# The closing projection of a two-layer decoder step: first halves of three chunks ahead, the last chunk's halves exchanged, and one more weight set in page buffers

## The chip, the cores and the metric

The kernel runs on one core of a Trainium2 chip. The metric is the device time of one execution in microseconds (us). Engines are named as in the profile: PE is TensorE (PEld its weight loads), DVE is VectorE, ACT is ScalarE, POOL is GpSimd, SP is SyncE, which here only issues DMAs.

## The reference

One inference step of a small decoder with two layers, on a prompt of 512 tokens and 8 sampled sequences of 8 new tokens, model width 1024. Layer 0 is a gated DeltaNet, layer 1 a differential attention over shared keys and values. What matters here is the last thing that is computed, the output projection of layer 1 with its gated residual:

```
def diff_mixer(h, k_all, v_all, ...):
    q, z = jnp.split(h @ w_in, [DIFF_WIDTH], axis=-1)
    ...
    o = rms_norm(o, sub_gain) * (1.0 - lam_init)
    o = o * jax.nn.silu(z.astype(F32)).reshape(b, L, DIFF_HEADS, DIFF_VH)
    return o.reshape(b, L, DIFF_WIDTH).astype(h.dtype) @ w_out

# run_group, layer 1
x = x + gate[:, None, :] * y
```

The matrix `w_out` is 1024 x 1024, and 512 + 64 = 576 tokens go through it.

## The kernel before, in words

Activations lie transposed: partitions are model components, columns are tokens. The 576 columns are cut in two halves of 288: half 0 is prompt tokens 0 to 287; half 1 is prompt tokens 288 to 511 (224 columns) and the 64 sample tokens. A matrix of 1024 x 1024 is cut into 8 chunks m of 128 outputs, and each chunk is a sum over 8 blocks k of 128 inputs; for the output projection, block k is head k.

Float32 products are made of three float32r products. Weights and activations are each split into a high part (a cast) and a low part (the value less the high part): `hhi` and `hlo` for activations, and a weight set of `whi` and `wlo` for a chunk. For each k, `run_part` issues hi x hi, hi x lo and lo x hi, so a half chunk is 24 matmuls of 288 columns into one PSUM bank.

A weight set j is loaded raw by SP into one of two `wraw` buffers (`weights`). Then `split_w` casts it on ACT (L2025) and subtracts twice 512 columns on POOL (L2031), or on DVE for some sets that the change does not touch. Where the two parts go is a table: for most late sets it is a slot of the room "w2", which has two, and which comes free when the chunk that uses it is done. Sets named in `OVER` go to two page buffers `pg`, which held key and value pages of the cache and which are no longer needed then. The closing projection uses sets 40 to 47; chunk m uses set 40 + m.

The activations of the closing projection come from `gated2`: for each head the attention output is multiplied by the gate (L2677, DVE), cast to `hhi` (L2682, ACT) and subtracted to `hlo` (L2684, DVE). It sets ("g", h, half) for the prompt part, and ("gs", 1) for the sample part of all heads, which comes from `samples_end`. So half 0 of a chunk needs ("g", k, 0), and half 1 needs ("g", k, 1) and ("gs", 1).

`out_second` (L2800) is the closing projection. It goes through a list `order` of (m, half). The first `HELD` entries are held: their blocks k 0 to 6 are issued first, each into its own bank, and the blocks k 7 of all of them after that, since head 7 is the last to be done. The other entries follow one after another. Banks go round in the order of `names`: pq, px, px, po, sc, sc, pt2, pv. `xin` loads the residual input for each entry of `order` into one of three `scr` buffers (L2812). `evac` adds the product times the gate (one DVE operation for half 0, three for half 1: `resid`, L1829, L1833, L1835) and stores the result (L2826); its buffer comes free when the store has landed. Half 1 leaves the weight set.

What sets the order of instructions on an engine is not this text alone. All pieces of work are generators that are driven by a planner (`Second.drive`) with costs for each step. It takes the step that can start first by its own clock, and by rank where two are equal; the order that it finds is then pinned on PE, ACT, DVE, POOL and SP. Each engine takes its instructions in that order, and each waits for what it needs.

Of the kernel before, what the change touches and what calls it, by code (L numbers as in the profile page):

```python
# [170 lines left out]
def scr(K, n):  # L171
    t = K.scr.tile([128, 640], F32, name="scr")
    return t[:, 0:n]
# [714 lines left out]
SPARE = 1.4  # L888
HALF = 8, 20
PAGES_AT = 1, 7  # L890
HELD = 4
EV = 3
BURST = 4
MORE = 2
OVER = 40,
CH = 3
PB = 3

# [925 lines left out]
def resid(K, pool, half, ps, m, gate_kt, xin, xout):  # L1824

    nc = K.nc
    g = K.mod[:, gate_kt + m, :]
    n = HT if half == 0 else SEQ - HT
    nc.vector.scalar_tensor_tensor(out=xout[:, :n], in0=ps[:, :n], scalar=g[:, 0:1], in1=xin[:, :n],  # L1829
                                   op0=ALU.mult, op1=ALU.add)  # L1830
    if half:
        t = pool.tile([128, NB, DS], F32, name="rst")
        nc.vector.tensor_mul(out=t[:], in0=ps[:, n:HT].rearrange("p (b e) -> p b e", e=DS),  # L1833
                             in1=g[:, 1:9].unsqueeze(2).to_broadcast([128, NB, DS]))
        nc.vector.tensor_add(out=xout[:, n:HT], in0=xin[:, n:HT], in1=t[:].rearrange("p b e -> p (b e)"))  # L1835
# [162 lines left out]
def weights(W, K, first, n, slot):  # L1998


    for j in range(first, first + n):
        room = "w" if j < 24 else "wx" if j == 26 and EV > 2 else "pg" if j in OVER else "w2"
        yield None, 0, Room("raw")
# [32 lines left out]
def run_part(W, K, j, ps, half, ks, step=2, conds=lambda k: ()):  # L2036

    ks = list(ks)
    for i in range(0, len(ks), step):
        now = ks[i:i + step]  # L2040
        yield "E", None, ("w", j), *[c for k in now for c in conds(k)]
        w = W.sets[j]
        for k in now:
            for a, b in ((0, 0), (0, 1), (1, 0)):
                K.mm(out=ps[:, :HT], lhsT=w[a][:, k, :], rhs=(K.hhi, K.hlo)[b][:, k, half * HT:half * HT + HT],
                     start=(k == 0 and a + b == 0), stop=(k == 7 and a == 1))
# [307 lines left out]
def second_projections(W, K):  # L2354
# [75 lines left out]
    yield from tile_row(W, K, [Tile2(W, K, "v", h) for h in range(8)], 24, "v", [nothing] * 2)  # L2430
    yield from tile_row(W, K, [Tile2(W, K, "z", h) for h in range(8)], 32, "z", named("hz"))
    yield from out_second(W, K)


# [365 lines left out]
def out_second(W, K):  # L2800


    P = W.P
    order = [(m, half) for m in range(8) for half in range(2)]
    xs = {}

    def xin():
        for m, half in order:
            yield None, 0, Room("scr"), ("z", 7, 0), ("z", 7, 1)
            t = scr(K, HT)  # L2810
            xs[m, half] = t, W.took[0]
            K.nc.sync.dma_start(out=t, in_=K.x1d[:, m, CUTS[half]])  # L2812
            W.load("S", 0.5, "xo", m, half)
            W.set("xol", m, half)

    def evac(m, half, bank):
        nc = K.nc
        ps, took = bank
        yield None, 0, ("xol", m, half)
        x, xr = xs[m, half]  # L2820
        yield "D", 0.52 if not half else 0.9, ("xo", m, half)
        y = x
        resid(K, P.ss, half, ps, m, 56, x, y)
        W.leave(took)
        yield None, 0
        nc.sync.dma_start(out=K.yT[:, m, CUTS[half]], in_=y)  # L2826
        W.load("S", 0.5, "yo", m, half)
        yield None, 0, ("yo", m, half)
        W.leave(xr)

    W.add(6, xin())
    def conds(half):
        return lambda k: (("g", k, half),) + ((("gs", 1),) if half else ())
    held = []
    names = ["pq", "px", "px", "po", "sc", "sc", "pt2", "pv"]
    for (m, half), name in zip(order[:HELD], names):
        yield None, 0, Room(name), *((("gs", 1),) if name in ("px", "po") else ())
        bank = getattr(K, name).tile([128, 512], F32, name=name), W.took[0]
        yield from run_part(W, K, 40 + m, bank[0], half, range(7), conds=conds(half))
        held.append(bank)  # L2840
    for (m, half), bank in zip(order[:HELD], held):
        yield from run_part(W, K, 40 + m, bank[0], half, (7,), conds=conds(half))
        W.add(0, evac(m, half, bank))
        if half:
            W.leave(*W.sets[40 + m][2])
    for i, (m, half) in enumerate(order[HELD:]):
        name = names[(i + HELD) % 8]
        yield None, 0, Room(name)
        bank = getattr(K, name).tile([128, 512], F32, name=name), W.took[0]
        yield from run_part(W, K, 40 + m, bank[0], half, range(8), conds=conds(half))  # L2850
        W.add(0, evac(m, half, bank))
        if half:
            W.leave(*W.sets[40 + m][2])
# [368 lines left out]
```

## Time and profile before

| | |
|---|---|
| runs | 1150.34, 1156.87, 1158.28 us; median 1156.87 |
| span of the profiled execution | 1149.0 us; its own device time is not listed apart from the span, and the lowest run is 1.3 us above it |
| busy share of the span | PE 97%, DVE 60%, ACT 60%, POOL 38% |
| granted TensorE clock | 0.995 on average |
| chain that ended last | PE 78%, ACT 7%, DVE 5%, DMA 5% |
| last matmul | starts at 1144.83 us of the span |

In the timelines a row is: start, duration, engine, line, operation, output <- inputs, shapes, and in brackets the idle time of the engine before it and what ended that. Names of tiles are without their numbers there, and the bank pt2 is printed as pt. In a table of windows each engine has its busy time in the window with the number of its instructions; then come the granted clock (1.00 is full), the busy share of the DMA engines and GB/s.

### The profile page before, as it was taken

How to read it: one execution, taken by the hardware profiler on the slowest of the kernel's cores; microseconds unless marked ns; L12 is line 12 of the kernel's file. 1: busy time of each engine (PE TensorE's matmuls, PEld its weight loads, DVE VectorE, ACT ScalarE, POOL GpSimd, SP SyncE). 2: the span in 40 equal slices, each digit the busy share in tenths (PEclk: the TensorE clock that was granted, in tenths of full speed). 3: DMA queues.
4: the chain of work that ended last, by engine and by line, in shares of the span. 5: the costliest groups of instructions: out<-in, count | busy, mean ns of one | idle time of the engine just before them, and what ended most of it. 6: DMA issues, size and time to landing. Idle time of an engine off the chain costs nothing.

```text
span 1149.0 us, 32501 instructions
## 1 busy us (share of the span) xinstructions
PE 1118.5 (97%) x12651; PEld 1036.0 (90%) x12651; DVE 694.6 (60%) x1803; ACT 693.9 (60%) x1901; POOL 439.4 (38%) x752
## 2 busy tenths in 40 slices
PE   8999999999999999999999999999999999999998
PEld 6899998999989998998989999999998888888988
DVE  4677875777777675866743657564433456555522
ACT  4666867777777867677753434685553566665510
POOL 3443433323334334232223432389962223422412
PEclk9999999999999999999999999999999999999989
DMA  9886565767657675686886889322589988988434
GB/s 366 214 231 165 143 199 133 192 155 198 166 139 192 145 206 142 179 215 163 234 239 160 273 287 341 124 59 74 182 305 328 312 295 324 317 275 302 154 99 125
DMA packets 87643, 239.97 MB, mean 209 GB/s; under 512 B 14450, under 2 KB 28658, under 8 KB 87490
## 3 DMA queue, kind: packets, MB, share of 16 engines
q1 hardware_dynamic: 71938, 181.27, 46.5%
q0 software_dynamic: 15552, 56.63, 22.6%
q8 instruction: 100, 1.64, 0.6%
q14 instruction: 53, 0.43, 0.1%
HBM read 212.02 MB, written 25.84 MB: 207 GB/s over the span
## 4 chain that ended last, share of the span: by engine, by line
PE 78%; ACT 7%; DVE 5%; DMA 5%; issue 3%; POOL 2%; SPq 1%; POOLq 0%; ACTq 0%; DVEq 0%
PE pp L271 24%; PE pp L1930 12%; PE pc L271 7%; PE pq L1930 7%; PE px L1930 4%; PE po L1930 3%; PE pa L271 3%; PE sc L1930 3%; PE pt L1935 3%; PE pt L271 3%; PE pt L1930 2%; PE pv L1930 2%; PE ps L271 2%; DMA whi<-wall 2%; PE pt L285 1%
## 5 line engine op out<-in xcount | busy, mean ns | idle before, releaser
L271 PE MATMUL pp<-hlo,whi 128*128 128x288 f32 x592 | 170.6, 309 | 0.0
L271 PE MATMUL pp<-hhi,whi 128*128 128x288 f32 x592 | 162.1, 294 | 0.0
L2031 POOL TENSOR_TENSOR wlo<-wraw,whi 128x512 fp32r<-128x512 f32 x80 | 108.6, 1371 | 137.5 <-ACT whi L2025 131.5
L1930 PE MATMUL pp<-hhi,whi 128*128 128x288 f32 x432 | 133.0, 309 | 2.4 <-DVE rst L1833 1.7
L1930 PE MATMUL pp<-hlo,whi 128*128 128x288 f32 x432 | 127.2, 295 | 0.0
L1930 PE MATMUL pp<-hhi,wlo 128*128 128x288 f32 x432 | 125.6, 295 | 0.0
L271 PE MATMUL pp<-hhi,wraw 128*128 128x288 f32 x576 | 123.8, 298 | 0.0
L271 PEld LDWEIGHTS pp<-hlo,whi 128*128 128x128 f32 x592 | 111.5, 188 | 1.8 <-issue 1.4
L271 PEld LDWEIGHTS pp<-hhi,whi 128*128 128x128 f32 x592 | 111.6, 188 | 0.5
L271 PE MATMUL pp<-hhi,wlo 128*128 128x288 f32 x592 | 103.5, 303 | 0.0
L271 PEld LDWEIGHTS pp<-hhi,wraw 128*128 128x128 f32 x576 | 94.0, 189 | 1.0 <-issue 0.4
L1930 PEld LDWEIGHTS pp<-hhi,whi 128*128 128x128 f32 x432 | 81.4, 188 | 6.8 <-issue 4.5
L1134 DVE SCALAR_TENSOR_TENSOR y<-u,vec,y 128x600 f32<-128x600 f32 x96 | 80.7, 841 | 9.4 <-ACT y L1131 8.7
L271 PEld LDWEIGHTS pp<-hhi,wlo 128*128 128x128 f32 x592 | 84.6, 188 | 0.8 <-issue 0.2
L271 PE MATMUL pp<-hlo,wraw 128*128 128x288 f32 x288 | 84.4, 314 | 0.1
L1930 PEld LDWEIGHTS pp<-hlo,whi 128*128 128x128 f32 x432 | 81.5, 189 | 0.0
L1930 PEld LDWEIGHTS pp<-hhi,wlo 128*128 128x128 f32 x432 | 80.8, 188 | 0.0
L2025 ACT CAST whi<-wraw 128x1024 fp32r<-128x1024 f32 x46 | 48.2, 1049 | 51.1 <-PE po L1930 18.1
L926 POOL DMA_DIRECT2D wlo<-wall x36 | 32.0, 890 | 118.7 <-ACT wlo L921 74.8
L2490 POOL COPY pg<-ptt 1x1 int32<-1x1 int32 x128 | 27.3, 224 | 125.8 <-PE po L1930 45.5
L1930 PE MATMUL pq<-hhi,whi 128*128 128x288 f32 x200 | 65.0, 325 | 0.6 <-ACT vch L2247 0.4
L1930 PE MATMUL pq<-hlo,whi 128*128 128x288 f32 x200 | 58.9, 295 | 0.0
(492 smaller groups left out, 3127.2 us busy)
## 6 DMA issues: line engine op xcount, KB each, us to landing
pg<-ck SPq DMA_DIRECT2D x64, 512.0 KB, 5.3
pg<-cv SPq DMA_DIRECT2D x64, 512.0 KB, 5.3
wraw<-wall SPq DMA_DIRECT2D x49, 512.0 KB, 4.4
wraw<-wall POOLq DMA_DIRECT2D x36, 512.0 KB, 6.0
whi<-wall POOLq DMA_DIRECT2D x36, 512.0 KB, 5.9
wlo<-wall POOLq DMA_DIRECT2D x36, 512.0 KB, 5.9
araw<-ada SPq DMA_DIRECT2D x24, 512.0 KB, 4.2
araw<-ada SPq DMA_DIRECT2D x8, 1024.0 KB, 13.8
```

The lines of the kernel that those rows point to most:

```text
L271: return self.K.nc.tensor.matmul(**kw)
L285: return self.K.nc.tensor.transpose(**kw)
L926: K.nc.gpsimd.dma_start(out=lo[:], in_=src, accum_op=ALU.add)
L1134: nc.vector.scalar_tensor_tensor(out=y[:, :YW], in0=u[:, j:j + YW], scalar=cw[j], in1=y[:, :YW], op0=ALU.mult, op1=ALU.add)
L1930: return self.K.nc.tensor.matmul(**kw)
L1935: return self.K.nc.tensor.transpose(**kw)
L2025: nc.scalar.copy(out=hi[:], in_=raw[:])
L2031: (nc.vector if shared else nc.gpsimd).tensor_sub(out=lo[:, q:q + 4], in0=raw[:, q:q + 4], in1=hi[:, q:q + 4].bitcast(F32))
L2490: nc.gpsimd.tensor_copy(out=e, in_=P.ptt[0:1, i:i + 1])
```

## The change

Four places, all in the closing projection and its tables. Three entries are held, not four, and they are the first halves of chunks 0, 1 and 2; their second halves follow. The last chunk's second half comes ahead of its first half. The banks go round in another order, and the two sc banks are taken only when the prompt's last attention product is issued (("pv", 7, 3)); the px and po banks no longer ask for ("gs", 1) themselves, while the second halves still wait for it. Set 43 goes to page buffers as set 40 does. Since no held entry is a second half, the release of a weight set goes from that loop.

```
-HELD = 4
+HELD = 3
...
-OVER = 40,
+OVER = 40, 43
...
-    order = [(m, half) for m in range(8) for half in range(2)]
+    order = [(m, half) for half in range(2) for m in range(HELD)] + [(m, half) for m in range(HELD, 7) for half in range(2)] + [(7, 1), (7, 0)]
...
-    names = ["pq", "px", "px", "po", "sc", "sc", "pt2", "pv"]
+    names = ["pq", "sc", "sc", "px", "px", "po", "pt2", "pv"]
     for (m, half), name in zip(order[:HELD], names):
-        yield None, 0, Room(name), *((("gs", 1),) if name in ("px", "po") else ())
+        yield None, 0, Room(name), *((("pv", 7, 3),) if name == "sc" else ())
         bank = getattr(K, name).tile([128, 512], F32, name=name), W.took[0]
         yield from run_part(W, K, 40 + m, bank[0], half, range(7), conds=conds(half))
         held.append(bank)
     for (m, half), bank in zip(order[:HELD], held):
         yield from run_part(W, K, 40 + m, bank[0], half, (7,), conds=conds(half))
         W.add(0, evac(m, half, bank))
-        if half:
-            W.leave(*W.sets[40 + m][2])
```

The order of instructions up to the middle of the closing projection's first chunk is the same on every engine. On PE, the first two blocks below begin with the end of chunk 0's first half up to head 6 (bank pq, set 40 in two pg tiles) and what follows it. Before, it is the second half of the same chunk:

```order
L1930 MATMUL pq_17218<-hhi_102,pg_17024 128x288
L1930 MATMUL pq_17218<-hlo_103,pg_17024 128x288
L1930 MATMUL pq_17218<-hhi_102,pg_17025 128x288
L1930 MATMUL px_17282<-hhi_102,pg_17024 128x288
L1930 MATMUL px_17282<-hlo_103,pg_17024 128x288
L1930 MATMUL px_17282<-hhi_102,pg_17025 128x288
```

Now it is the first half of chunk 1 (bank sc, set 41):

```order
L1930 MATMUL pq_17218<-hhi_102,pg_17024 128x288
L1930 MATMUL pq_17218<-hlo_103,pg_17024 128x288
L1930 MATMUL pq_17218<-hhi_102,pg_17025 128x288
L1930 MATMUL sc_17270<-hhi_102,whi_17169 128x288
L1930 MATMUL sc_17270<-hlo_103,whi_17169 128x288
L1930 MATMUL sc_17270<-hhi_102,wlo_17170 128x288
```

So 42 matmuls of sc, 21 for each of chunks 1 and 2, have come between pq and px. The second place on PE is where the held banks get head 7. Before, four are closed, and the first half of chunk 2 follows (bank sc, set 42):

```order
L1930 MATMUL pq_17218<-hhi_102,pg_17024 128x288
L1930 MATMUL pq_17218<-hlo_103,pg_17024 128x288
L1930 MATMUL pq_17218<-hhi_102,pg_17025 128x288
L1930 MATMUL px_17282<-hhi_102,pg_17024 128x288
L1930 MATMUL px_17282<-hlo_103,pg_17024 128x288
L1930 MATMUL px_17282<-hhi_102,pg_17025 128x288
L1930 MATMUL px_17304<-hhi_102,whi_17169 128x288
L1930 MATMUL px_17304<-hlo_103,whi_17169 128x288
L1930 MATMUL px_17304<-hhi_102,wlo_17170 128x288
L1930 MATMUL po_17326<-hhi_102,whi_17169 128x288
L1930 MATMUL po_17326<-hlo_103,whi_17169 128x288
L1930 MATMUL po_17326<-hhi_102,wlo_17170 128x288
```

Now three are closed, and only then comes the first second half, that of chunk 0 in bank px:

```order
L1930 MATMUL pq_17218<-hhi_102,pg_17024 128x288
L1930 MATMUL pq_17218<-hlo_103,pg_17024 128x288
L1930 MATMUL pq_17218<-hhi_102,pg_17025 128x288
L1930 MATMUL sc_17270<-hhi_102,whi_17169 128x288
L1930 MATMUL sc_17270<-hlo_103,whi_17169 128x288
L1930 MATMUL sc_17270<-hhi_102,wlo_17170 128x288
L1930 MATMUL sc_17307<-hhi_102,whi_17225 128x288
L1930 MATMUL sc_17307<-hlo_103,whi_17225 128x288
L1930 MATMUL sc_17307<-hhi_102,wlo_17226 128x288
L1930 MATMUL px_17345<-hhi_102,pg_17024 128x288
L1930 MATMUL px_17345<-hlo_103,pg_17024 128x288
L1930 MATMUL px_17345<-hhi_102,pg_17025 128x288
```

Head 7 has moved from behind 63 matmuls of second halves to behind 42 of first halves, and the first use of the sample columns to behind 51. On ACT, the piece of the difference at the end of its program (L2682 are the casts of activations, 8x64 the sample columns of all heads; L2025 are the casts of weight sets):

```order
 L2682 CAST hhi_102<-qT_9616 128x224 x7
 L2682 CAST hhi_102<-qT_9616 128x288
+L2025 CAST pg_17278<-wraw_17212 128x1024
 L2682 CAST hhi_102<-qT_9616 128x8x64
 L2682 CAST hhi_102<-qT_9616 128x224
-L2025 CAST whi_17366<-wraw_17212 128x1024
-L2025 CAST whi_17436<-wraw_17272 128x1024
-L2025 CAST whi_17505<-wraw_17410 128x1024
-L2025 CAST whi_17575<-wraw_17481 128x1024
-L2025 CAST whi_17645<-wraw_17552 128x1024
```

Set 43's cast has moved from behind the last casts of activations to ahead of the sample columns' cast. On POOL its two subtractions have moved along. They follow those of set 42 as before, and wait for the cast. On DVE the order of the hlo subtractions is the same.

## The prediction

> **What bounds the kernel now.** The page first.
>
> ```profile
> span 1149.0 us, 32501 instructions
> PE 1118.5 (97%) x12651; PEld 1036.0 (90%) x12651; DVE 694.6 (60%) x1803; ACT 693.9 (60%) x1901; POOL 439.4 (38%) x752
> PEclk9999999999999999999999999999999999999989
> PE 78%; ACT 7%; DVE 5%; DMA 5%; issue 3%; POOL 2%; SPq 1%; POOLq 0%; ACTq 0%; DVEq 0%
> ```
>
> TensorE is busy for 97% of the span and is 78% of the chain that ended last. The change keeps all its matmuls, so it can win only where TensorE stands still or runs slowly, and behind its last matmul. There is one clock slice below 9, the last but one. Next the list of TensorE's waits, by what ended them (total, times, longest):
>
> ```profile
> PE px L1930 <- ACT hhi L2682: 3.7, 1, 3.7
> PE px L1930 <- DVE hlo L2684: 0.3, 1, 0.3
> ```
>
> The longest single wait of the kernel, and a short one right behind it, lie at bank px, the second half of chunk 0, which needs the sample columns of hhi and hlo. The timeline of TensorE around it, to its end (start, duration), and the same stretch in windows (us, busy time of PE, PEld, DVE, ACT, POOL, then clock and DMA):
>
> ```profile
> 1089.97 0.29 PE L1930 MATMUL pq<-hhi,pg 128*128 128x288 f32 x1
> 1093.95 0.61 PE L1930 MATMUL px<-hhi,pg 128*128 128x288 f32 x1 [3.68 <-ACT hhi L2682]
> 1094.87 0.61 PE L1930 MATMUL px<-hlo,pg 128*128 128x288 f32 x1 [0.32 <-DVE hlo L2684]
> ...
> 1099.46 0.29 PE L1930 MATMUL px<-hhi,pg 128*128 128x288 f32 x1
> 1099.59 0.29 PE L1930 MATMUL px<-hhi,whi 128*128 128x288 f32 x1
> ...
> 1144.83 0.29 PE L1930 MATMUL pv<-hhi,wlo 128*128 128x288 f32 x1
> ```
>
> ```profile
> 1090.10:1092.45 2.35, 0.16 (x2) 0.00 (x0) 2.35 (x5) 0.22 (x1) 0.73 (x1) 1.00 0.25 37
> 1092.45:1099.28 6.83, 5.01 (x19) 4.70 (x20) 2.67 (x7) 0.90 (x2) 0.00 (x0) 0.50 0.18 64
> 1099.28:1145.12 45.84, 45.84 (x346) 45.61 (x344) 10.33 (x29) 5.24 (x5) 12.67 (x10) 1.00 0.42 126
> ```
>
> From the first px chunk after the gap to the end there are 342 matmuls by the code (21 of (1,0), 21 of (1,1), 12 that close the four held chunks, 12 x 24): 1099.59 to 1144.83 is 45.24 us for 341 steps, **0.1327 us a matmul**, without a wait. The idle stretch also brought the clock down: 0.50 for 6.83 us. So the closing projection is TensorE alone, at full pace except at that one place.
>
> **What the gap costs.** At full pace the matmul behind 1089.97 would start at 1090.10. It starts at 1093.95, which is 3.85 late. The next starts 0.92 behind it, so 0.79 over a step. From there to 1099.46 are 19 steps in 4.59 us, where full pace needs 2.52: 2.07 for the half clock. Together **6.71 us**.
>
> **What the change puts there.** Ahead of px now stand 42 matmuls of the first halves of chunks 1 and 2 (k 0 to 6) and nine that close the three held chunks. Their operands: first-half columns of k 0 to 6 were read by pq already. The lower part of set 42 is the later weight: the POOL rows below end at 1090.83, and PE comes to that set after 21 steps, at 1092.89. The condition that ("pv",7,3) be done only delays the sc banks to the end of the prompt's attention; its conversions are what pq just read. So 42 steps run from 1090.10 without a wait, then the first of chunk 0's k 7 starts at 1095.67, and the second, which reads hlo of head 7, could start at 1095.81.
>
> **What the change adds in the gap.** Set 43 goes to two page buffers, so its cast on ScalarE now stands between the last first-half cast and the sample cast, and its two POOL subtractions fall in the gap.
>
> ```profile
> 1084.83 0.34 SPq L2006 DMA_DIRECT2D wraw<-wall  x1
> wraw<-wall SPq DMA_DIRECT2D x2, 512.0 KB, 3.7
> 1086.99 1.04 ACT L2025 CAST whi<-wraw 128x1024 fp32r<-128x1024 f32 x1
> 1089.89 0.43 ACT L2682 CAST hhi<-qT 128x288 fp32r<-128x288 f32 x1
> 1093.28 0.90 ACT L2682 CAST hhi<-qT 128x512 fp32r<-128x512 f32 x2 [2.95 <-DVE qT L2677]
> ```
>
> ScalarE is idle for 2.95 us there. The raw weights, issued at 1084.83 with 3.7 us to landing, are in at about 1088.5. The cast runs from 1090.32 to 1091.36 and ends before the sample cast can start, 1093.28. On ScalarE it costs nothing. On POOL and VectorE it does not hide, and this I take from the timeline of set 42, whose subtractions met the same VectorE work:
>
> ```profile
> 1088.11 1.33 POOL L2031 TENSOR_TENSOR wlo<-wraw,whi 128x512 fp32r<-128x512 f32 x1 [1.14 <-ACT whi L2025]
> 1088.34 1.35 DVE L2684 TENSOR_TENSOR hlo<-qT,hhi 128x224 fp32r<-128x224 f32 x1
> 1089.40 1.43 POOL L2031 TENSOR_TENSOR wlo<-wraw,whi 128x512 fp32r<-128x512 f32 x1
> 1089.61 1.46 DVE L2684 TENSOR_TENSOR hlo<-qT,hhi 128x224 fp32r<-128x224 f32 x1
> 1091.66 0.37 DVE L2684 TENSOR_TENSOR hlo<-qT,hhi 128x224 fp32r<-128x224 f32 x1
> 1093.77 0.45 DVE L2684 TENSOR_TENSOR hlo<-qT,hhi 128x288 fp32r<-128x288 f32 x1
> 1094.14 0.68 DVE L2684 TENSOR_TENSOR hlo<-qT,hhi 128x512 fp32r<-128x512 f32 x1
> ```
>
> Alone an hlo subtraction of 224 columns takes 0.37. Beside a POOL subtraction it takes 1.35 and 1.46, ending 0.25 behind it. Two held ones cost 1.35 + 1.46 - 2 x 0.37 = 2.07 us (the same figure as the half clock by chance). The new POOL pass starts at about 1091.44 and lies over the hlo operations from 1091.66 on, so I shift that whole chain by 2.07: hlo of head 7 is done at 1094.22 + 2.07 = 1096.29 and its matmul starts 0.05 later (1094.82 to 1094.87 above), at 1096.34, against 1095.81. **TensorE waits 0.53 us.** That is far from the 2.35 us of idling (1090.10 to 1092.45) after which the clock fell, so it stays at 1.00. Behind it come eight steps, so px starts at 1097.40; the sample cast (first of the two in its row, which with the shift are done at 1096.25) and its hlo (1094.82 + 2.07 = 1096.89) are there. Bounds: 0 if the two passes do not meet, and 1.4 if each costs a full 1.46 (2 x 1.46 = 2.92, 0.85 more than 2.07).
>
> The Trainium skill, page "SBUF — State Buffer", section "SBUF: two separate sides", says that a VectorE operation with two SBUF inputs and a GpSimd operation exclude each other, whichever starts first keeping the shared ports for its whole instruction. It speaks against placing set 43's subtractions here, and the rows agree (1.35 and 1.46 instead of 0.37). By that rule the sum has the 0.53, without it the gain would be 0.53 larger.
>
> **What is moved and costs nothing.** SP's load of set 45 now stands ahead of the first stores and waits for set 43's subtractions (about 1094.2); the first evacuation can start when the hlo chain is done, at about 1097.2 (1094.82, one more of 0.37, and the 2.07), and its store after that, so nothing queues behind it. Later sets are released one after another as before: the cast waiting at 1106.94 in the first row below feeds a chunk at 1113.10, over 6 us on. The residual input has three buffers, and VectorE waits for its loads, but behind eight banks:
>
> ```profile
> 1106.94 1.05 ACT L2025 CAST whi<-wraw 128x1024 fp32r<-128x1024 f32 x1 [12.77 <-PE po L1930]
> 1113.10 0.30 PE L1930 MATMUL pt<-hhi,whi 128*128 128x288 f32 x1
> DVE scr L1829 <- DMA scr<-x1d: 17.1, 5, 5.0
> 1105.76 0.52 DVE L1829 SCALAR_TENSOR_TENSOR scr<-pq,mod,scr 128x288 f32<-128x288 f32 x1 [10.64 <-PE pq L1930]
> 1110.91 0.45 DVE L1829 SCALAR_TENSOR_TENSOR scr<-po,mod,scr 128x224 f32<-128x224 f32 x1 [3.45 <-DMA scr<-x1d]
> 1121.64 0.52 DVE L1829 SCALAR_TENSOR_TENSOR scr<-pt,mod,scr 128x288 f32<-128x288 f32 x1 [4.60 <-DMA scr<-x1d]
> 1129.44 0.45 DVE L1829 SCALAR_TENSOR_TENSOR scr<-px,mod,scr 128x224 f32<-128x224 f32 x1 [4.96 <-DMA scr<-x1d]
> ```
>
> Evacuation 0 starts at 1105.76 and evacuation 9 at 1129.44, 2.63 us a chunk even where loads held it, against 24 x 0.1327 = 3.18 of TensorE. Started at 1097.2, fifteen more end up at 1136.7, before the last matmul.
>
> **The end of the kernel.** Chunk 7's second half comes first, so behind the last matmul stands one VectorE operation, not three.
>
> ```profile
> 1145.16 0.45 DVE L1829 SCALAR_TENSOR_TENSOR scr<-pv,mod,scr 128x224 f32<-128x224 f32 x1 [2.68 <-PE pv L1930]
> 1145.78 0.23 DVE L1835 TENSOR_TENSOR scr<-scr,rst 128x64 f32<-128x64 f32 x1
> 1146.03 0.33 SPq L2826 DMA_DIRECT2D o_y<-scr  x1
> ```
>
> Now 1145.16 to 1146.01 is 0.85; a first half takes 0.52 (the rows of 1105.76 and 1121.64 above). **0.33 us** less. The store is of the same size, so what follows stays.
>
> **Sum.** 6.71 - 0.53 + 0.33 = 6.51 us. The profiled execution would have a span of 1149.0 - 6.5 = 1142.5, with the last matmul starting at 1144.83 - 6.18 = 1138.65. The runs before are 1150.34, 1156.87 and 1158.28, so the span is 1.3 below the lowest and 7.9 below the median; their spread, 7.94, is larger than the gain. What varies there is not in the profile, so I take the gain off the median: **1150.4 us**, 0.56% less.
>
> **The rivals.**
> First, the half clock is not there in each run. In the profile it begins 2.35 us into the gap, which is 1.5 us before work returns; had it begun later than that, 2.07 of the gain would be absent: 4.4 us, 1152.4. For it: one execution is seen. Against it: the clock did fall, with time to spare. The Trainium skill, page "TensorE: Matmul & The Clock Gate", Part 1, states free-running windows of 3413 ns and a fall after at least one idle window. The half stretch of 6.83 us is two windows, which agrees; but it fell after 2.35 us of idling, which is less than one, so the rule as worded does not hold here. By it a gap of 3.85 us would hold a whole window only in few runs, and most would show this rival. The one row that is seen speaks for the fall, so the rival has 0.20.
>
> Second, the gap comes back: ScalarE takes its queue in order, so a late raw load of set 43 now holds the sample cast. The slowest kind of load on the page bounds it:
>
> ```profile
> araw<-ada SPq DMA_DIRECT2D x8, 1024.0 KB, 13.8
> ```
>
> 13.8 us from 1084.83 is 1098.63, cast 1099.67, sample cast 0.62 of it more, 1100.3, hlo 0.7 later: px at 1101.0 instead of 1097.4. That is 3.6 lost, and an idle time as long as today's takes the half clock along, 2.07 more: a gain of 0.8, 1156.0. It decides from a landing after some 1095, since cast, sample cast and hlo then end behind px's place. Against: 3.7 measured. 0.07.
>
> Third, slower: the evacuation through three buffers becomes the bound. From evacuation 3 (1110.91) to 6 (1121.64) three chunks took 10.73. If SP's new order of stores, loads and weights kept that pace all along, five such turns from 1097.2 end at 1150.9 instead of 1145.16, 5.7 later, less 0.3: 1162.3. To lose at all it takes 9.6 a turn ((1145.16 - 1097.2) / 5), to show at all 8.3 ((1138.9 - 1097.2) / 5). Against: 2.63 a chunk is 7.9 a turn, and the long one held two weight loads. 0.05. That the change does not do what it says is excluded by the order of instructions; only the clock's part can be missing.
>
> **How the numbers follow.** Forecast 0.68, first rival 0.20, second 0.07, third 0.05. The range: the lowest run less the largest gain, 1150.34 - 7.04 (no hold of VectorE) = 1143.3, to the second rival's 1156.0; rounded 1143 to 1156, which also covers the first rival on the highest run (1158.28 - 4.4 = 1153.9). About 1%, 11.6 us, is what a measurement of this kernel can tell from no change. No case gains that much by itself; only the spread of the runs, 0.7%, added to 0.56% does: 0.13. Slower by over 1% needs the third rival at a worse pace than seen, or that spread on top: 0.03. Within 1%: 0.84.
>
> **What would show it.** In the profile after: no TensorE wait on ACT hhi of 3.7 and a clock of 1.00 from 1090 to the last matmul; 42 sc matmuls from 1090.10; one wait of about half a microsecond at pq on DVE hlo; two hlo operations of 1.3 to 1.5 us beside POOL rows on pg near 1091.5 to 1094.2; px near 1097.4; the last matmul near 1138.65 and one VectorE operation of 0.52 behind it. A wait of pq or px over 2 us, a clock of 0.50 there, or TensorE waiting for VectorE on a bank behind 1100 would prove the forecast wrong.

## The result, and the profile after

The changed kernel takes **1144.32 us** (median of 7 runs, 1142.17 to 1145.79) against 1154.26 us of the kernel before in the same comparison (7 runs, 1148.32 to 1158.28). The ratio of the times is 0.9928, with a 95% interval of 0.9907 to 0.9949. A second comparison of the same two kernels gave 1144.51 us (12 runs, 1142.22 to 1150.35) against 1150.29 us (17 runs, 1147.55 to 1156.07), ratio 0.9946 [0.9927, 0.9965]. So the change gains something more than half a per cent, with intervals that run from 0.35% to 0.93%: by the ratios 8.3 us in the first comparison and 6.2 in the second. (The medians alone lie 9.9 and 5.8 us apart.) The predicted time was 1150.4 us, with a range of 1143 to 1156.

The profiled execution of the changed kernel took 1145.45 us, 1.75 us more than its span. The same lines of its page as were shown of before:

```profile
span 1143.7 us, 32504 instructions
PE 1118.4 (98%) x12651; PEld 1036.8 (91%) x12651; DVE 697.5 (61%) x1803; ACT 693.5 (61%) x1901; POOL 439.7 (38%) x752
PEclk9999999999999999999989999999999999999999
```

TensorE does the same work (1118.4 us busy, 12651 instructions) in a span that is 5.3 us shorter. The clock slice below 9 has left the end of the kernel, and there is one in the middle that was not there before; more on it below. The list of TensorE's waits (total, times, longest):

```profile
PE pa L271 <- ACT V L1673: 2.2, 2, 1.8
PE pq L1930 <- DVE hlo L2684: 0.3, 1, 0.3
```

The wait of 3.7 us at px on ACT hhi is gone. In its place stands one short wait at pq on DVE hlo, as forecast. The other row is a wait in the middle of the kernel that had been 0.5 us long. TensorE's timeline around the former gap and at the end, with VectorE's last operation:

```profile
1091.21 0.29 PE L1930 MATMUL pq<-hhi,pg 128*128 128x288 f32 x1
1091.35 0.30 PE L1930 MATMUL sc<-hhi,whi 128*128 128x288 f32 x1
...
1096.90 0.29 PE L1930 MATMUL pq<-hhi,pg 128*128 128x288 f32 x1
1097.46 0.40 PE L1930 MATMUL pq<-hlo,pg 128*128 128x288 f32 x1 [0.27 <-DVE hlo L2684]
...
1098.62 0.30 PE L1930 MATMUL px<-hhi,pg 128*128 128x288 f32 x1
...
1139.91 0.29 PE L1930 MATMUL pv<-hhi,wlo 128*128 128x288 f32 x1
1140.24 0.52 DVE L1829 SCALAR_TENSOR_TENSOR scr<-pv,mod,scr 128x288 f32<-128x288 f32 x1 [2.33 <-PE pv L1930]
```

Behind the last first-half step of chunk 0 the sc bank follows 0.14 us later, where before there was a hole to 1093.95. The held chunk's second step on block 7 starts 0.56 behind the first, so 0.43 over the normal step of 0.133. The windows (us, busy time of PE, PEld, DVE, ACT, POOL, then clock and DMA) show that nothing else is left:

```profile
1087.67:1091.35 3.68, 3.68 (x32) 3.68 (x31) 2.91 (x4) 3.42 (x10) 2.54 (x3) 1.00 0.67 239
1091.35:1097.46 6.11, 5.84 (x46) 5.61 (x44) 6.11 (x10) 2.06 (x4) 3.43 (x3) 1.00 0.42 127
1097.46:1098.62 1.16, 1.16 (x8) 1.16 (x9) 1.16 (x3) 0.00 (x0) 0.00 (x0) 1.00 0.58 233
1098.62:1139.91 41.29, 41.29 (x314) 41.29 (x312) 9.49 (x31) 4.20 (x4) 10.15 (x8) 1.00 0.41 127
```

The clock is 1.00 in every row, and behind px TensorE is busy for 41.29 of 41.29 us.

To compare executions I use one stretch, called **S** from here on: from the first matmul of chunk 0's first half to the end of the last matmul. Its TensorE window, of the kernel before and of the kernel after:

```profile
1086.42:1145.12 58.70, 54.70 (x394) 0.94 0.40 122
```

```profile
1087.67:1140.20 52.53, 52.26 (x394) 1.00 0.43 136
```

S is 58.70 before and 52.53 after, **6.17 us** less; what follows the last matmul went from 3.88 us (1149.0 - 1145.12) to 3.50 (1143.7 - 1140.20), **0.38** less. Together 6.55. The two spans differ by only 5.3 because the closing stage began 1.25 us later in the profiled execution after (1087.67 against 1086.42). Most of that comes from one place, 500 us earlier, in TensorE's windows and timeline of the same execution:

```profile
580.60:584.01 3.41, 1.57 (x13) 1.00 0.89 343
584.01:587.43 3.42, 3.42 (x23) 0.50 0.87 160
587.43:590.84 3.41, 3.41 (x16) 0.50 0.89 273
```

```profile
583.93 1.92 PE L271 MATMUL pa<-WF,V 64*64 64x64 f32 x16 [1.84 <-ACT V L1673]
```

A wait on ScalarE was 1.84 us long there, and TensorE ran at half clock for two windows behind it. In the profiled execution of before the wait at this place was 0.51 and the clock stayed up. Compared matmul by matmul, the execution after is 0.9 us ahead of that of before at 573 us and 3.1 behind it at 618; some 2 us of that are made up further on, still ahead of the closing projection. The change doesn't touch that stage, and the repeated execution of the changed kernel (below) has 1.19 there and no half clock. It belongs to the execution, not to the change.

### The profile page after: what moved, and what is told of

It is laid out like the page before. It is cut to its first block, busy times and chain, and to the rows that moved or that the text cites. A ratio compares the mean times of both kernels' runs of the same rounds, so it can differ in the third digit from the quotient of the medians.

```text
span 1143.7 us, 32504 instructions
## 1 busy us (share of the span) xinstructions
PE 1118.4 (98%) x12651; PEld 1036.8 (91%) x12651; DVE 697.5 (61%) x1803; ACT 693.5 (61%) x1901; POOL 439.7 (38%) x752
## 4 chain that ended last, share of the span: by engine, by line
PE 78%; ACT 7%; DVE 5%; DMA 4%; issue 3%; POOL 2%; SPq 1%; POOLq 0%; ACTq 0%; DVEq 0%
PE pp L271 24%; PE pp L1930 12%; PE pc L271 7%; PE pq L1930 7%; PE px L1930 4%; PE po L1930 3%; PE pa L271 3%; PE pt L1935 3%; PE pt L271 3%; PE sc L1930 2%; PE pt L1930 2%; PE pv L1930 2%; PE ps L271 2%; DMA whi<-wall 2%; PE pt L285 1%
## 5 line engine op out<-in xcount | busy, mean ns | idle before, releaser
L2031 POOL TENSOR_TENSOR wlo<-wraw,whi 128x512 fp32r<-128x512 f32 x78 | 106.3, 1376 | 128.7 <-ACT whi L2025 117.1
L2025 ACT CAST whi<-wraw 128x1024 fp32r<-128x1024 f32 x45 | 47.2, 1049 | 42.9 <-PE px L1930 13.1
L1930 PE MATMUL pq<-hhi,wlo 128*128 128x288 f32 x200 | 58.9, 295 | 0.0
```

Source lines behind the costliest of these rows:

```text
L1930: return self.K.nc.tensor.matmul(**kw)
L2025: nc.scalar.copy(out=hi[:], in_=raw[:])
L2031: (nc.vector if shared else nc.gpsimd).tensor_sub(out=lo[:, q:q + 4], in0=raw[:, q:q + 4], in1=hi[:, q:q + 4].bitcast(F32))
```

## The experiments

The theory: the gain is the gap's 6.71 us (a wait of 3.85 and 0.79, and 2.07 for the half clock that follows it), less a new wait of 0.53 for the subtractions of set 43, and 0.33 from the exchange at the end. The rivals: that the half clock is not there in each execution; that set 43 in page buffers costs or brings something else; that the exchange takes part in the gap.

**The exchange alone.** In the kernel before:

```
-    order = [(m, half) for m in range(8) for half in range(2)]
+    order = [(m, half) for m in range(7) for half in range(2)] + [(7, 1), (7, 0)]
```

> The kernel before, with only the last chunk's halves exchanged. Measure: S, from the first pq matmul of chunk 0 to the end of the last matmul (58.70 us before, 52.53 after), and the tail from there to the end of the span (3.88 before, 3.49 after). Theory (cover of the gap, and apart from it a shorter tail): S stays 58.7 with the gap and the half clock, the tail falls by 0.3 to 0.4, to 3.5; the time by as much, which one run cannot show. Rival (the exchange is part of what closed the gap): S falls too, by more than 0.5.

One run took 1150.14 us. TensorE's windows of the gap, and the end in the timeline:

```profile
1089.44:1092.86 3.42, 0.07 (x1) 1.00 0.46 133
1092.86:1096.27 3.41, 2.76 (x10) 0.50 0.05 20
1096.27:1099.69 3.42, 3.42 (x16) 0.50 0.00 0
```

```profile
1144.60 0.29 PE L1930 MATMUL pv<-hhi,wlo 128*128 128x288 f32 x1
1144.93 0.52 DVE L1829 SCALAR_TENSOR_TENSOR scr<-pv,mod,scr 128x288 f32<-128x288 f32 x1 [2.33 <-PE pv L1930]
```

The tail is 3.51 us (span 1148.4 less 1144.89), as short as in the changed kernel: the exchange is worth 0.37, and is alone responsible for that part. The gap and the half clock are still there, and S is 59.22 (1085.67 to 1144.89), not less than before's 58.70. So the exchange has no share in the gap.

**Set 43 back in the ordinary slots.** In the changed kernel:

```
-OVER = 40, 43
+OVER = 40,
```

> The changed kernel with OVER as before, so set 43 waits for a weight slot again. Theory (set 43's subtractions hold VectorE's hlo in the gap, and buy nothing): no hlo operation over 0.5 us behind the first two, no TensorE wait at pq on hlo, S = 52.53 - 0.53 = 52.0, and no wait at the first use of set 43, since its first half of low parts is there about 0.8 us earlier. Rival (the page buffers are needed): TensorE waits 1 us or more for set 43 or 44, S above 53.5.

1145.9 us (12 runs, 1142.56 to 1150.68) against 1152.76 of before (23 runs), ratio 0.9933 [0.991, 0.9957]. From the timeline and TensorE's share of S:

```profile
1092.58 0.98 DVE L2684 TENSOR_TENSOR hlo<-qT,hhi 128x224 fp32r<-128x224 f32 x3
...
1087.32:1139.35 52.03, 52.03 (x394) 51.80 (x392) 17.84 (x45) 9.78 (x17) 15.94 (x13) 1.00 0.45 137
```

Three hlo subtractions take 0.98 together, and TensorE is busy for all of S. S is 52.03, 0.50 less than in the changed kernel: what the wait for set 43 was forecast to cost (0.53). The page buffers for that set buy nothing in S in return. The rest of the gain is there without them. Half a microsecond lies within the interval of the times, so only the trace tells these two kernels apart.

**Four first halves ahead.** In the changed kernel:

```
-HELD = 3
+HELD = 4
```

> The changed kernel with four first halves held, not three: 63 matmuls ahead of head 7, so it is reached at about 2.8 us later than in the changed kernel. Theory (what is left is only the wait of half a microsecond for hlo of head 7, which more cover hides): no wait at pq, S = 52.0. Rival (the order of the rest or the banks set the pace): S 52.5 or more, with new waits on banks or on set 44.

1144.24 us (6 runs, 1142.07 to 1146.32) against the same 1152.76, ratio 0.9913 [0.9881, 0.9945].

```profile
1094.35 2.90 DVE L2684 TENSOR_TENSOR hlo<-qT,hhi 128x224 fp32r<-128x224 f32 x3
...
1089.09:1141.06 51.97, 51.97 (x394) 51.74 (x392) 20.02 (x45) 9.69 (x17) 16.09 (x13) 1.00 0.44 137
```

VectorE is held as in the changed kernel (2.90 for three subtractions, not 0.98), but 21 more matmuls stand ahead of the step that needs them, and the wait is gone: S is 51.97. With 52.03 of the run above this gives the floor of S, **52.0 us**, reached in two ways. Either version is the better by half a microsecond in the trace, and the times cannot show it.

**Two first halves ahead.** `HELD = 2` at the same place, so 21 matmuls fewer cover the gap.

> The changed kernel with two first halves held, not three: 21 matmuls ahead of head 7, not 42. Theory (the gain is the length of the cover, up to where hlo of head 7 is ready, 9.8 us after the first pq matmul in the changed kernel's profile): TensorE waits 3.2 us at pq; with 340 steps of 0.1327 us left from there, S = 9.8 + 45.1 + 0.3 = 55.2 if the clock holds, and 58 to 58.6 if an idle time of 3.2 us brings the half clock. Rival (the order itself, not its length, is what counts): S 52 to 53.

One run took 1148.37 us. From the timeline, and TensorE's windows:

```profile
1096.06 0.40 PE L1930 MATMUL pq<-hlo,pg 128*128 128x288 f32 x1 [3.02 <-DVE hlo L2684]
```

```profile
1093.31:1096.72 3.41, 0.66 (x5) 1.00 0.58 166
1096.72:1100.13 3.41, 3.41 (x17) 0.50 0.28 102
1086.29:1143.07 56.78, 53.76 (x394) 0.97 0.41 126
```

With too little cover the gap is back, at pq now, with a wait of 3.02 and with the half clock. S is 56.78: between the 55.2 expected without the half clock and the 58 to 58.6 with it, since the half clock held for 3.41 us and not for 6.83.

**The gap without its half clock.** The kernel before, with 28 matmuls on data that are there already, issued in the gap into the free sc bank, their result unread:

```
+        if (m, half) == (0, 1):
+            yield None, 0, Room("sc"), ("pv", 7, 3)
+            room, = W.took
+            idle = K.sc.tile([128, 512], F32, name="sc")
+            yield "E", None, ("w", 40)
+            for _ in range(28):
+                K.mm(out=idle[:, :HT], lhsT=W.sets[40][0][:, 0, :], rhs=K.hhi[:, 0, 0:HT], start=True, stop=True)
+            W.leave(room)
```

> The kernel before, with 28 matmuls of 288 columns on a free sc bank, whose result nobody reads, issued between pq and px: the wait for the sample columns stays and TensorE is kept busy through it. 28 x 0.1327 = 3.7 us. Theory (of the 6.71 us, 2.07 are the half clock that the idle time brings, 4.64 the wait): clock 1.00 over the stretch, the px matmuls at 0.133 apart, S = 58.70 - 2.07 = 56.6, the time 2 us below before. Rival (the slow px matmuls have another cause, such as the operands just written): they stay at 0.24 apart, S 58.7, no change of time.

1150.15 us (12 runs, 1144.7 to 1155.62) against 1152.76, ratio 0.9973 [0.995, 0.9995]: 3.1 us less, with an interval of 0.6 to 5.8. S from the windows:

```profile
1085.17:1141.92 56.75, 56.20 (x422) 55.53 (x420) 17.94 (x43) 9.79 (x17) 16.00 (x13) 1.00 0.41 127
```

The kernel does 28 matmuls more than before and is faster. The clock is 1.00 for all of S, and S is 56.75. Above the floor that leaves 4.75 us, which is the price of the late sample columns alone (forecast 3.85 + 0.79 = 4.64); the 1.95 between 56.75 and before's 58.70 is the half clock (forecast 2.07).

**Half the filling.** The same with `range(14)`.

> As the kernel with 28 matmuls on an unread bank between pq and px, but with 14, 1.86 us: an idle time of about 2 us is left, then the 0.8 us between the first two px matmuls. If the clock needs more idle time than the 2.2 to 3.3 us after which it fell in the two profiles that have the gap, it holds here: S = 56.7. If less idle time in its window is enough, it falls: S 58 or more.

One run took 1151.8 us. The rest of the gap in the timeline, and in TensorE's windows:

```profile
1096.98 0.40 PE L1930 MATMUL px<-hhi,pg 128*128 128x288 f32 x1 [1.86 <-ACT hhi L2682]
1097.90 0.40 PE L1930 MATMUL px<-hlo,pg 128*128 128x288 f32 x1 [0.52 <-DVE hlo L2684]
```

```profile
1092.89:1096.31 3.42, 2.23 (x17) 1.00 0.40 120
1096.31:1099.72 3.41, 2.22 (x14) 1.00 0.08 34
```

1.86 and 0.52 us of idling stayed without a half clock; S is 56.75 again. The run's longer time is from elsewhere: its closing stage began at 1089.44, 3 to 4 us later than in the others of before's kind, with 13.65 us of half clock ahead of it. How much of the delay comes from the half clock isn't separated.

**The kernel before, two more executions with a profile.**

> The kernel before, unchanged, for another profile. If the clock falls in the gap in each execution (forecast), there is a half clock of 6.8 us there and S is 58.2 to 59.3, as in the two profiles so far (58.70, 59.22). If it depends on the execution (first rival of the prediction), S is 56.7 without it.

> The kernel before, unchanged, once more, with the same expectations: S 58.2 to 59.3 with the half clock in the gap, 56.7 without it.

Both took 1149.44 us, with S of 58.27 (1085.59 to 1143.86) and 58.22 (1085.62 to 1143.84). TensorE's windows of the first and of the second:

```profile
1087.41:1090.82 3.41, 2.02 (x17) 1.00 0.25 83
1090.82:1094.23 3.41, 0.59 (x2) 1.00 0.41 154
1094.23:1097.64 3.41, 3.41 (x15) 0.50 0.00 0
```

```profile
1090.56:1093.97 3.41, 0.40 (x1) 1.00 0.43 154
1093.97:1097.38 3.41, 3.31 (x14) 0.50 0.00 0
```

The clock fell in both, but only after work had come back (at 1093.12 and 1093.14), and for 3.41 us instead of 6.83. In all four profiled executions that have the full gap (before, these two, and the one with the exchange alone) it fell: S is 58.70, 58.27, 58.22 and 59.22.

**The changed kernel once more**, in the second comparison told of at the top.

> The changed kernel, unchanged, timed again: the traces give 5.7 to 6.7 us for the closing projection (S 58.2 to 59.2 in four profiles with the gap, 52.53 in the changed one) and 0.4 for the tail, 6.1 to 7.1 together, a ratio of about 0.9943. The first comparison gave 0.9928 (0.9907 to 0.9949). If the traces hold all of the gain, the ratio comes out at 0.993 to 0.996; if there is more to it than the closing projection, at 0.992 or less. S 52.5.

```profile
1084.48:1136.97 52.49, 52.23 (x394) 1.00 0.45 137
```

S is 52.49 and the tail 3.53 (1140.5 - 1136.97): the changed stretch repeats to 0.04 us. The mean S of the kernel before over its three profiled executions is 58.40, of the changed kernel 52.51 over two: 5.89 less. The tails were 3.88, 3.84 and 3.86 before and are 3.50 and 3.53: 0.35 less. Together 6.24 us, which is 0.54% of 1150.29. The second comparison measured just that (0.9946). The first one's 8.3 us are 2 more; 6.24 of 1154.26 would be a ratio of 0.9946, which lies inside its interval.

## Why the prediction was right, point by point

**The gap, 6.71 us.** Right. Before's 58.70 less the floor of 52.0 is 6.7. Its parts were forecast as 4.64 for the wait and 2.07 for the clock, and filling the gap separated them into 4.75 and 1.95.

**The half clock in each execution (first rival, given 0.20).** It fell in all four profiles, so the rival's price was not paid. The rival had named a condition, that the half clock begins only after work has returned, and expected none of the 2.07 to be gained then. That condition did hold in two of the four, by 1.1 and 0.8 us, and the half clock still cost about 1.5: the condition was the wrong one, and the forecast stood all the same. Beyond the profiles, each run lists its mean granted clock: in 40 runs of the kernel before in two comparisons it was at most 0.999, and a single stretch of 3.41 us at half clock gives 0.9985 (1 - 0.5 x 3.41 / 1149); of the 49 runs of the four kernels without a half clock in S (the changed one, set 43 in the slots, four ahead, the gap filled) 7 reached 1.000. This fits a fall in each run of before and does not prove it, since the mean counts half clock at other places too. What the prediction had not seen is that the size varies: from S, the half clock cost 1.5 (58.22 - 56.75) to 2.5 (59.22 - 56.75), and the profiled execution stood between.

**The new wait, 0.53.** Right in place, mechanism and size. The rows of POOL and VectorE, from the timeline after:

```profile
1092.59 1.29 POOL L2031 TENSOR_TENSOR pg<-wraw,pg 128x512 fp32r<-128x512 f32 x1 [0.49 <-ACT pg L2025]
1092.93 1.20 DVE L2684 TENSOR_TENSOR hlo<-qT,hhi 128x224 fp32r<-128x224 f32 x1
1093.84 1.44 POOL L2031 TENSOR_TENSOR pg<-wraw,pg 128x512 fp32r<-128x512 f32 x1
1094.05 1.47 DVE L2684 TENSOR_TENSOR hlo<-qT,hhi 128x224 fp32r<-128x224 f32 x1
```

Two subtractions of set 43, and two of hlo that take 1.20 and 1.47 beside them (forecast 1.35 and 1.46, and 1.3 to 1.5 as the sign to look for, which the first just misses), with 0.98 / 3 = 0.33 each where POOL is elsewhere. The step at pq was 0.43 late, and S shrinks by 0.50 when the set goes back to the slots and by 0.56 with more cover. The rule of the Trainium skill that the prediction set beside this, from the page "SBUF — State Buffer", section "SBUF: two separate sides" (whichever of the two starts first keeps the shared ports for its whole instruction), agrees with these rows: the first hlo operation ends 0.25 behind POOL's first (1094.13 and 1093.88).

**The end, 0.33.** It was 0.38, and 0.37 with the exchange alone.

**What was moved and costs nothing.** TensorE has no wait behind px, and no wait on set 43 or 44. Set 43's raw load came in time: its cast ran at 1091.47, and the sample cast began at 1096.46, so the second rival (a late load holds the sample cast) did not occur. For the third rival (three buffers of the evacuation as the bound) the list of waits has VectorE's on the loads of the residual input, now 11.2 us in 3 times where it was 17.1 in 5:

```profile
DVE scr L1829 <- DMA scr<-x1d: 11.2, 3, 4.4
```

No bank was late from it.

**The marks.** Shifted by the 1.25 us by which the stage began later, sc was forecast at 1091.35, px at 1098.65 and the last matmul at 1139.90; they stand at 1091.35, 1098.62 and 1139.91.

**From the sum to the time.** This is the step that was weak. The prediction took the gain off the median of the three runs that it had, 1156.87, and said that what varies between runs is not in the profile. With more runs the kernel before has medians of 1154.26 (seven, those three among them), 1150.29 and 1152.76, so 1156.87 was a high sample. The forecast time came out 6.1 us above the measured one: 2.6 of it is the base (1156.87 less 1154.26), and the rest is that the medians of this comparison lie 9.9 apart, where 6.51 was forecast and the traces show 6.24. The time lies in the range because its lower end was taken off the lowest run and not off the median. From the second comparison's base, 1150.29, the same gain of 6.51 gives 1143.8, where 1144.51 was measured.

What varies between runs is in part to be seen in the granted clock. Half a clock over a stretch would take half of its length if TensorE were busy all through it, so by this estimate 0.001 of the mean clock over 1149 us is 1.15 us. In the 23 runs of before in the comparison of the experiments, time and mean clock go together (correlation -0.79), with a slope of 1.19 us per 0.001; the correlation leaves about 40% of the variance (1 - 0.79 squared = 0.38) for something else. It is not so everywhere. The 17 runs of before in the second comparison have -0.69 and 0.91 us, the 12 with the gap filled -0.44 and 0.67. Of the 12 runs of the changed kernel in the second comparison, one has a mean clock of 0.946, which would be 62 us, and is only 6 slower than their median; in the other 11 time and clock do not go together (-0.05). The profiled one among them has 10.24 us of half clock at 13.84 and is the fastest of the twelve (1142.22). So the mean clock alone does not give the time, and what a stretch of half clock costs seems to depend on its place, which was not tried.

## What to carry to other kernels

A wait of TensorE is paid for twice: its length, and the half clock that a long one brings down behind it (here 4.75 and about 2 us). Both go if enough independent matmuls stand between the last operand that is there and the one that is late; count the cover in matmuls times pitch, and let the work that produces the late operand stand free of passes on POOL, which cost 0.5 us of S here and brought nothing in it. Before subtracting a gain from a median of three runs, see how far that median can move: here it went from 1156.87 to 1150.29 with other runs, which is as much as the whole gain. And to judge a change of one stage, measure that stage in several traces, as with S here, which repeated to 0.04 us in the changed kernel.

## What the runs showed of the hardware that was not expected

**The half clock comes on a fixed raster within an execution.** Its stretches, those cut off by the end of the execution aside, are 3.41, 6.83 or 10.24 us long, and their starts fit one raster of 3.413 us over the whole execution: in the kernel before they are at 13.84, 1092.45 and 1147.06, and 1078.61 and 54.61 are 316 and 16 times 3.4133 to within 0.01. Likewise after (13.99 and 584.01) and with four ahead (12.88, 456.61 and 589.73). The raster's offset differs from execution to execution. It agrees with what the Trainium skill says on the page "TensorE: Matmul & The Clock Gate", Part 1, of free-running windows of 3413 ns.

**A window need not be idle altogether.** The clock was decided at a window's end, whatever happened at that instant, which is why it fell in the middle of idling or after work was back. TensorE's windows of before ahead of its fall in the gap and of the one at 1147.06, behind the last matmul, and one with set 43 in the slots, behind which the clock stayed up:

```profile
1089.04:1092.45 3.41, 1.22 (x10) 1.00 0.25 53
1143.65:1147.06 3.41, 1.47 (x12) 1.00 0.08 29
1137.60:1141.01 3.41, 1.75 (x14) 1.00 0.18 66
```

In the closing stage the windows ahead of a fall were busy for 1.47, 1.22, 0.66, 0.59, 0.40 and 0.07 us of 3.41; windows with 1.75, 2.02, 2.22 and 2.23 (all shown here or above) brought no fall. The limit lies between 1.47 and 1.75 for these matmuls of 128 x 128, as far as these show. In this stage it went back up behind a window at half clock that was busy for 3.31 us or more; behind 2.76 (the exchange alone) it stayed down for one more. Elsewhere that is not enough: the window from 584.01 after, shown at the top, was busy for all of its 3.42 us, and the clock stayed down for one more. This fits that the half clock of the gap held for 3.41 us where work was back early in the window and for 6.83 where it wasn't. So the same wait can be cheap or dear by its place on the raster: the 1.86 and 0.52 us of the half filling were cut by a window's border into two windows that were each busy enough. Whether it would have fallen with another offset was not tried.

**In other stages a busy share does not sort it.** With small matmuls (64 x 64), in the stage that waits on ScalarE near 454 us, these rows are from the timelines of before, of the kernel with the gap filled, and of the one with four ahead:

```profile
455.07 1.14 PE L271 MATMUL pa<-XA,ckq 64*64 64x64 f32 x16 [1.50 <-ACT WF L1660]
```

```profile
454.28 1.14 PE L271 MATMUL pa<-XA,ckq 64*64 64x64 f32 x16 [1.62 <-ACT WF L1660]
```

```profile
454.80 1.14 PE L271 MATMUL pa<-XA,ckq 64*64 64x64 f32 x16 [1.26 <-ACT WF L1660]
```

The first brought no half clock, the other two did, within 2 us. The window around this place, in the two further executions of before:

```profile
452.53:455.94 3.41, 1.91 (x20) 1.00 0.01 2
452.26:455.68 3.42, 1.93 (x23) 1.00 0.27 30
```

Behind the first the clock stayed up; behind the second it fell, though TensorE was busy for as long. With four ahead the window was busy for 2.15 us, more than in either, and the clock fell too. What counts as activity there, and whether these matmuls count less than those of 128 x 128, stays open.
